# Modulation products half a tile behind their loads, the loads tied to the unit of weights at hand, and the gates' second bank from the common group

## The chip, the cores and the metric

The kernel runs on one core of one Trainium2 chip. The metric is device time in microseconds (us). Time before: 2287.91 us, the median of three runs (2285.56 to 2290.13). Engines are called as the profile calls them: PE (matrix products), PEld (its weight loads), DVE (elementwise), ACT (activations and casts), POOL (here small copies and the issue of some transfers) and SP (the issue of most transfers).

## The reference, cut to what matters

One layer works on 512 latent tokens x and 256 context tokens ctx, both of width 2048. A modulation vector is made from c by a matrix product with a large weight, `w_mod` (2048 x 12288). The normalised, modulated input goes through one combined projection `w_in`. Group A of its columns feeds a gated linear attention over chunks, forward and backward, whose start states come from the context; group B feeds a short convolution. Both are joined and go through an output projection, and a feed-forward block follows.

```python
m = silu(c) @ w_mod + b_mod          # six vectors of 2048: shift, scale, gate, twice
h = modulate(rmsnorm(x, norm1_g), shift1, scale1)
q, k, v, g, lf, lb, cb, cc, cx = split_proj(h @ w_in)
la_f = log_sigmoid(lf @ w_gate_f + b_gate_f) / 16     # la_b alike
o, _, _ = gla_bidir(q, k, v, la_f, la_b, s0_f, s0_b)  # s0 from the context tokens
x = x + gate1 * (concat(norm(o) * silu(g), cb * conv(cc * cx)) @ w_out)
x = x + gate2 * swiglu(modulate(rmsnorm(x, norm2_g), shift2, scale2))
```

Only the first two of the six vectors (4096 columns) are needed before the projection. The other 8192 columns of `w_mod`, 64 tiles of 128 rows by 2048, are worked off beside the projection and the attention, and are needed only after it.

## The kernel before, in words

**A unit of weights.** Weights of 32-bit floats are used as a high and a low part. A unit is 128 x 1024 numbers, 512 KB. `load_w` (from L125) loads it into a buffer of the group `raw` (L119 to L123, four buffers, issued by SP), ACT casts it to `whi` (L106), DVE subtracts to get `wlo` (L107); `whi` and `wlo` have three buffers each. `mm3` (L96) makes each product of three matmuls, so a unit is 24 matmuls of 128 x 512 in `proj_units` (from L499), which also remembers the present unit's `whi` in `unit`. Two units fill one accumulator.

**The modulation products.** `mod_some` (L380 to L409) works on the 128 half tiles, of 128 x 1024 and 512 KB each, of the rest of `w_mod`. For each, one transfer and one product with the broadcast silu(c) on DVE (L405), whose sum over the row is accumulated into a column of `modacc`, are written down. `behind` says how many half tiles the products stand behind their loads. At 0 the load takes a `raw` buffer on SP's queue, and the product is written right behind it. Above 0 the load is issued by POOL (L393, or L397), and ahead of it stands a copy of one column from the present unit's `whi` into the buffer (L392, or L396); the transfer overwrites it. The copy thus makes the transfer wait until that unit has been cast. Two thirds of these half tiles take one of two `wm` buffers, the others a `raw` buffer.

**The order of the work.** Code order sets each engine's queue, and a framework puts in the waits; each engine works its queue in order. `weave` (L564 to L570) takes stages in turn: one step of the stages, one unit of weights, then `mod_some` for 1.84 half tiles on the average.

- The context's states: `do_ctx` (from L518, six stages) with the four units of `do_q(0)` and `do_q(1)` (weights `wq`). Its last stages copy the start states (L551), on ACT or DVE as the framework chooses. Eleven half tiles, m0 to m10, are written here.
- The gates: `do_gates` (from L582), four stages tt0 to tt3. Each makes two gate tiles on PE in two banks `pzs` (forward, backward); `log_gates` (L489) then has ACT work through L493, L494 and L495, and DVE make the log gates (L497), which frees the banks. Beside them run the units of `do_g(0)` (four units of `wg`, G1 to G4) and `do_conv(0)` (from L681, six units of `wc`, C1 to C6). Eighteen half tiles, m11 to m28.
- The attention, head by head (`do_gla`, from L590), with the other units. Ahead of it stands `behind[0] = 2` (L705), so here POOL issues the transfers of half tiles.

The product of half tile mN is called pN below. The banks of 128 x 512 come from two groups: `bank` has five and `abank` three. The accumulators of the units are from `abank`, and so is the second `pzs` of a gate stage (L584).

Of the kernel before, what the change touches and what calls it, by code (L numbers as in the profile page):

```python
# [53 lines left out]
def tile_hybrid_block(  # L54
# [23 lines left out]
    def big(dtype=F32):  # L78
        return xpool.tile([P, SEQ], dtype, tag="t", name="big")
# [4 lines left out]
    def bank(name="bank"):  # L84
        return pspool.tile([P, 512], F32, tag="g", name=name, bufs=5)

    def abank(name="abank"):
        return pspool.tile([P, 512], F32, tag="a", name=name, bufs=3)
# [4 lines left out]
    def mm(o, l, r, start, stop):  # L93
        nc.tensor.matmul(o, l, r, start=start, stop=stop, skip_group_check=True)  # L94
# [24 lines left out]
    def load_raw(src):  # L119
        n = src.shape[-1]  # L120
        r = wpool.tile([P, 1024], F32, tag="raw", name="raw", bufs=4)
        nc.sync.dma_start(r[:, :n], src)
        return r[:, :n]  # L123
# [11 lines left out]
    def tok(t, tt):  # L135
        return t[:, tt * P : tt * P + P]
# [200 lines left out]
    def gate_rows(pz, half, d, a):  # L337

        q = slice(64 * half, 64 * half + 33)
        mm(pz, lfT[q, a : a + P], gatet[q, d, :], True, True)  # L340
# [35 lines left out]
    nmod, owed = [0], [0.0]  # L376

    pend, behind, unit = [], [0], []

    def mod_some(n, last):  # L380


        owed[0] += 2 * n
        while owed[0] >= 1 and (pend or nmod[0] < 2 * last):
            owed[0] -= 1
            if nmod[0] < 2 * last:
                j, hf = divmod(nmod[0], 2)
                src = wm2[j][:, hf * 1024 : hf * 1024 + 1024]
                if behind[0] and nmod[0] % 3:
                    w = gp.tile([P, 1024], F32, tag="wm", name="wm", bufs=2)  # L390

                    nc.gpsimd.tensor_copy(w[:, 0:1], unit[0])  # L392
                    nc.gpsimd.dma_start(w, src)  # L393
                elif behind[0]:
                    w = wpool.tile([P, 1024], F32, tag="raw", name="raw", bufs=4)
                    nc.gpsimd.tensor_copy(w[:, 0:1], unit[0])  # L396
                    nc.gpsimd.dma_start(w, src)  # L397
                else:
                    w = load_raw(src)
                pend.append((j, hf, w))  # L400
                nmod[0] += 1
                if len(pend) <= behind[0]:
                    continue
            j, hf, w = pend.pop(0)
            nc.vector.tensor_tensor_reduce(  # L405
                out=w, in0=w, in1=cbc[:, hf * 1024 : hf * 1024 + 1024], scale=1.0, scalar=0.0,
                op0=ALU.mult, op1=ALU.add, accum_out=modacc[:, j, hf : hf + 1])
# [81 lines left out]
    def log_gates(pool, tag, pzs, las):  # L489

        t = pool.tile([P, 2, 512], F32, tag=tag, name="lg")
        for i in range(2):
            nc.scalar.activation(t[:, i, :], pzs[i], AF.Abs)  # L493
        nc.scalar.activation(t, t, AF.Exp, scale=-1.0)  # L494
        nc.scalar.activation(t, t, AF.Ln, bias=onecol)  # L495
        for i in range(2):
            nc.vector.scalar_tensor_tensor(las[i], pzs[i], 0.0, t[:, i, :], op0=ALU.min, op1=ALU.subtract)  # L497

    def proj_units(acc, wsrc, x, units=(0, 1), part=ALL):  # L499

        for n, u in enumerate(units):
            w = load_w(wsrc[u], 8)
            unit[:] = [w[0][:, 0, 0:1].bitcast(F32)]
            for k in range(8):
                mm3(acc[:, part], sl(w, ALL, k), sl(x[8 * u + k], ALL, part), n == 0 and k == 0, n == 1 and k == 7)
            yield
# [5 lines left out]
    def do_q(h):  # L512
        acc = abank("acc")
        yield from proj_units(acc, wq[h], hx)
        q_t[h] = big()
        nc.scalar.activation(q_t[h], acc, AF.Copy, scale=QSCALE)

    def do_ctx():  # L518
        kds = [[], []]
        las = []  # L520
        for d in range(2):
            pzs = [bank("pzs") for _ in range(NCT)]
            for tt in range(NCT):
                gate_rows(pzs[tt], tt, d, SEQ + tt * P)
            las.append([big() for _ in range(NCT)])
            log_gates(hcpool, "lg", pzs, las[d])
            yield
        for d in range(2):
            for tt in range(NCT):
                pz = bank("pz")  # L530
                whole = tt == d
                mm(pz, cstt[:, B_SUFF + d, :], las[d][tt], True, not whole)
                if whole:
                    mm(pz, one16, las[d][1 - tt], False, True)
                tag, bufs = (("sq0", 2), (("lfs", "tm")[tt], 1))[d]
                e = hcpool.tile([P, 512], F32, tag=tag, name="kdc", bufs=bufs)
                nc.scalar.activation(e, pz, AF.Exp)
                nc.vector.tensor_tensor(e, e, kc[tt], op=ALU.mult)
                kds[d].append(e)
            yield  # L540
        S0[:] = [xpool.tile([P, 2, DV], F32, tag="t", name="s0") for h in range(HEADS)]
        for d in range(2):
            for hp in range(2):
                pz = bank("pz")
                for hh in range(2):
                    h = 2 * hp + hh
                    for tt in range(NCT):
                        mm(pz[:, hh * DV : hh * DV + DV], tok(kds[d][tt], h), vc[tt][hp][:, hh * DV : hh * DV + DV],
                           hh == 0 and tt == 0, tt == 1)
                for hh in range(2):  # L550
                    nc.any.tensor_copy(S0[2 * hp + hh][:, d, :], pz[:, hh * DV : hh * DV + DV])  # L551
            yield
# [11 lines left out]
    def weave(stages, fill):  # L564

        for _ in stages:
            next(fill, None)
            mod_some(MOD_STEP, 64)
        for _ in fill:
            mod_some(MOD_STEP, 64)  # L570

    weave(do_ctx(), (None for g in (do_q(0), do_q(1)) for _ in g))


# [6 lines left out]

    def do_gates():  # L582
        for tt in range(NX):
            pzs = [bank("pzs"), abank("pzs")]  # L584
            for d in range(2):
                gate_rows(pzs[d], d, d, tt * P)
            log_gates(hcpool, "lg", pzs, [las[0][tt], las[1][tt]])
            yield
# [92 lines left out]
    def do_conv(c):  # L681
# [17 lines left out]
        mix[8 + c] = y  # L699

    weave(do_gates(), (None for g in (do_g(0), do_conv(0)) for _ in g))
    es_hc.close()
    es_g = ExitStack()
    gp = es_g.enter_context(tc.tile_pool(name="gp", bufs=1, side="right"))
    behind[0] = 2  # L705
    for h in range(HEADS):
# [3 lines left out]
        if h + 2 < HEADS:  # L710
            fill.insert(0, do_q(h + 2))
        weave(do_gla(h), (None for g in fill for _ in g))
    mod_some(128, 64)
    mod_finish(0, 64)
    nc.vector.tensor_scalar(gsc2, modv[:, 32:48], 1.0, None, op0=ALU.add)
# [634 lines left out]
```

## Time and profile before

| what | us |
|---|---|
| median of three runs | 2287.91 (2285.56 to 2290.13) |
| the profiled execution, own time | 2285.08 |
| its span (first to last instruction) | 2283.3 |
| mean granted clock of PE | 0.996 |
| PE busy | 2233.8 (98%) |
| DVE busy | 1657.4 (73%) |
| ACT busy | 1003.3 (44%) |
| POOL busy | 248.4 (11%) |

The span is 1.8 us shorter than the execution's own time; the execution is 2.8 us under the median. In a row of the timeline stand the start in us from the span's start, the duration in us, engine, line, operation, what is written and read, sizes and a count; in square brackets the idle time of the engine just before it, and what ended it. In a row of the waits stand the engine, the tile and line that waited, who was waited for, the time in all, how often, and the longest. Matmuls overlap: their rows begin 0.23 us apart and are 0.39 us long.

### The profile page before, as it was taken

How to read it: one execution, taken by the hardware profiler on the slowest of the kernel's cores; microseconds unless marked ns; L12 is line 12 of the kernel's file. 1: busy time of each engine (PE TensorE's matmuls, PEld its weight loads, DVE VectorE, ACT ScalarE, POOL GpSimd, SP SyncE). 2: the span in 40 equal slices, each digit the busy share in tenths (PEclk: the TensorE clock that was granted, in tenths of full speed). 3: DMA queues.
4: the chain of work that ended last, by engine and by line, in shares of the span. 5: the costliest groups of instructions: out<-in, count | busy, mean ns of one | idle time of the engine just before them, and what ended most of it. 6: DMA issues, size and time to landing. Idle time of an engine off the chain costs nothing.

```text
span 2283.3 us, 28033 instructions
## 1 busy us (share of the span) xinstructions
PE 2233.8 (98%) x10276; PEld 1785.8 (78%) x10276; DVE 1657.4 (73%) x2069; ACT 1003.3 (44%) x1354; POOL 248.4 (11%) x396
## 2 busy tenths in 40 slices
PE   8999998999999999999999999999999999999997
PEld 4765666887788887777888888888888888888886
DVE  3566165565768646899788779878887887787885
ACT  3423155333233434665554455444545544433343
POOL 2433100222323000100000000000000000000000
PEclk9999999999999999999999999999999999999999
DMA  9683466565677354523643454354335596756752
GB/s 328 218 278 132 148 220 199 197 223 203 239 238 254 117 191 168 204 74 122 210 148 117 160 179 157 130 171 165 136 139 205 203 338 208 242 198 203 258 168 100
DMA packets 163410, 433.16 MB, mean 190 GB/s; under 512 B 18022, under 2 KB 38790, under 8 KB 163144
## 3 DMA queue, kind: packets, MB, share of 16 engines
q1 hardware_dynamic: 128984, 331.20, 43.4%
q0 software_dynamic: 22416, 78.66, 9.8%
q10 hardware_dynamic: 11872, 21.52, 2.5%
q8 instruction: 81, 1.33, 0.2%
q14 instruction: 57, 0.47, 0.1%
HBM read 380.95 MB, written 50.35 MB: 189 GB/s over the span
## 4 chain that ended last, share of the span: by engine, by line
issue 56%; POOL 2%; PE 1%; DVE 1%; ACT 0%; DMA 0%; POOLq 0%; DVEq 0%; ACTq 0%
POOL opd L1070 2%; PE acc L94 1%; DVE wlo L107 0%; DVE ch L849 0%; ACT y L1217 0%; DMA out<-g 0%; DVE u L1023 0%; POOL xnd L1026 0%; ACT whi L106 0%; POOL hbig L962 0%; DVE hbig L1024 0%; DVE u L869 0%; POOLq L1070 0%; ACT acc L1208 0%; DVE g L1205 0%
## 5 line engine op out<-in xcount | busy, mean ns | idle before, releaser
L106 ACT CAST whi<-ch 128x1024 fp32r<-128x1024 f32 x335 | 353.1, 1055 | 407.5 <-PE acc L94 343.3
L107 DVE TENSOR_TENSOR wlo<-ch,whi 128x1024 fp32r<-128x1024 f32 x335 | 407.6, 1221 | 122.7 <-ACT whi L106 121.9
L106 ACT CAST whi<-raw 128x1024 fp32r<-128x1024 f32 x258 | 271.0, 1052 | 455.9 <-PE acc L94 287.9
L107 DVE TENSOR_TENSOR wlo<-raw,whi 128x1024 fp32r<-128x1024 f32 x258 | 316.2, 1226 | 197.6 <-ACT whi L106 191.6
L94 PE MATMUL acc<-hhl,whi 128*128 128x512 f32 x640 | 199.1, 392 | 0.0
L94 PE MATMUL acc<-hhi,wlo 128*128 128x512 f32 x320 | 133.0, 417 | 11.8 <-DVE wlo L107 5.6
L94 PEld LDWEIGHTS acc<-hhl,whi 128*128 128x128 f32 x640 | 120.2, 188 | 27.3 <-issue 2.5
L1070 POOL DMA_DIRECT2D opd<-ol x80 | 43.3, 541 | 880.2 <-DVE ol L107 880.0
L405 DVE CUSTOM_DVE_ANT_0 wm<-wm,cbc 128x1024 f32<-128x1024 f32 x66 | 80.6, 1224 | 79.4 <-DMA wm<-wm 78.5
L94 PE MATMUL acc<-wlo,a6h 128*128 128x512 f32 (+1 forms) x330 | 127.4, 386 | 1.2 <-DVE wlo L107 1.2
L94 PE MATMUL acc<-wlo,a0h 128*128 128x512 f32 x324 | 127.5, 394 | 0.8 <-DVE wlo L107 0.8
L94 PE MATMUL acc<-whi,a6l 128*128 128x512 f32 (+1 forms) x330 | 127.1, 387 | 0.3 <-DVE v L869 0.3
L94 PE MATMUL acc<-whi,a6h 128*128 128x512 f32 (+1 forms) x330 | 127.2, 386 | 0.0
L94 PE MATMUL acc<-hhl,wlo 128*128 128x512 f32 x320 | 126.5, 395 | 0.0
L94 PE MATMUL acc<-whi,a5h 128*128 128x512 f32 x324 | 126.3, 390 | 0.0
L94 PE MATMUL acc<-hlo,whi 128*128 128x512 f32 x320 | 126.1, 394 | 0.2 <-DVE hlo L112 0.2
L94 PE MATMUL acc<-whi,a0h 128*128 128x512 f32 x324 | 126.2, 390 | 0.0
L94 PE MATMUL acc<-whi,a5l 128*128 128x512 f32 x324 | 126.2, 389 | 0.0
L94 PE MATMUL acc<-wlo,a5h 128*128 128x512 f32 x324 | 126.1, 389 | 0.0
L94 PE MATMUL acc<-whi,a0l 128*128 128x512 f32 x324 | 126.0, 390 | 0.0
L94 PE MATMUL acc<-hhi,whi 128*128 128x512 f32 x320 | 125.7, 393 | 0.0
L405 DVE CUSTOM_DVE_ANT_0 raw<-raw,cbc 128x1024 f32<-128x1024 f32 x62 | 75.4, 1222 | 49.0 <-DMA raw<-wm 48.8
(334 smaller groups left out, 4986.0 us busy)
## 6 DMA issues: line engine op xcount, KB each, us to landing
raw<-wu SPq DMA_DIRECT2D x92, 512.0 KB, 4.3
ch<-wu SPq DMA_DIRECT2D x88, 512.0 KB, 3.8
wm<-wm POOLq DMA_DIRECT2D x66, 512.0 KB, 5.4
raw<-wd SPq DMA_DIRECT2D x50, 512.0 KB, 5.8
raw<-wc SPq DMA_DIRECT2D x48, 512.0 KB, 4.9
opd<-oh ACTq DMA_DIRECT2D x80, 256.0 KB, 3.5
opd<-ol POOLq DMA_DIRECT2D x80, 256.0 KB, 3.9
ch<-wd SPq DMA_DIRECT2D x38, 512.0 KB, 4.3
```

What stands on the lines that cost most here:

```text
L94: nc.tensor.matmul(o, l, r, start=start, stop=stop, skip_group_check=True)
L106: nc.scalar.copy(hi, src)
L107: (eng or nc.vector).tensor_tensor(lo, src, hi, op=ALU.subtract)
L405: nc.vector.tensor_tensor_reduce(out=w, in0=w, in1=cbc[:, hf * 1024 : hf * 1024 + 1024], scale=1.0, scalar=0.0, op0=ALU.mult, op1=ALU.add, ...
L1070: nc.gpsimd.dma_start(opd[j][i, 1].rearrange("p k t -> p (k t)"), lo.bitcast(F32))
```

## The change

```diff
@@ mod_some @@
-                if behind[0] and nmod[0] % 3:
+                if behind[0] > 1 and nmod[0] % 3:
                     w = gp.tile([P, 1024], F32, tag="wm", name="wm", bufs=2)
...
                 elif behind[0]:
                     w = wpool.tile([P, 1024], F32, tag="raw", name="raw", bufs=4)
                     nc.gpsimd.tensor_copy(w[:, 0:1], unit[0])
                     nc.gpsimd.dma_start(w, src)
@@ ahead of the context's states @@
+    behind[0] = 1
     weave(do_ctx(), (None for g in (do_q(0), do_q(1)) for _ in g))
@@ do_gates @@
-            pzs = [bank("pzs"), abank("pzs")]
+            pzs = [bank("pzs") for _ in range(2)]
```

From the context's states to the attention `behind` is 1. The 29 loads m0 to m28 leave SP's queue for POOL's, each behind a copy from the present unit's `whi`; all still take `raw` buffers, of which there are four as before. Each product stands one half tile behind its load, p28 in the attention. The second bank of each gate stage comes from `bank`. Behind the new line all line numbers are one higher.

SP's queue in the gates' stages, of the kernel before: units (`wg`, `wc`) and half tiles (`wm2`).

```order
L122 DMA raw_2790<-wg 128x1024
L122 DMA raw_2820<-wm2 128x1024
L122 DMA raw_2823<-wm2 128x1024
L122 DMA raw_2837<-wg 128x1024
L122 DMA raw_2867<-wm2 128x1024
L122 DMA raw_2870<-wm2 128x1024
L122 DMA raw_2876<-wc 128x1024
```

The same place of the changed kernel, from G3 (`raw_2803`) on.

```order
L122 DMA raw_2803<-wg 128x1024
L122 DMA raw_2852<-wg 128x1024
L122 DMA raw_2893<-wc 128x1024
L122 DMA raw_2931<-wc 128x1024
L122 DMA raw_2972<-wc 128x1024
```

And POOL's queue there; in the kernel before POOL has nothing in this stretch. `whi_2805` is G3, `whi_2854` is G4, and `raw_2833` to `raw_2886` are m14 to m17.

```order
L396 COPY raw_2833<-whi_2805 128x1
L396 COPY raw_2837<-whi_2805 128x1
L397 DMA raw_2833<-wm2 128x1024
L397 DMA raw_2837<-wm2 128x1024
L396 COPY raw_2882<-whi_2854 128x1
L396 COPY raw_2886<-whi_2854 128x1
L397 DMA raw_2882<-wm2 128x1024
L397 DMA raw_2886<-wm2 128x1024
```

The half tiles moved from SP to POOL, mostly in pairs, each pair behind the cast of the unit then at hand; SP's queue holds units alone.

DVE's queue ahead of the log gates of tt0 (the two rows of L497), before: `raw_2820` to `raw_2909` are m14 to m19, `wlo_2793` is G3. The short instruction that reads the sum out behind each product is left out here and below.

```order
L405 ISA raw_2820,modacc_76<-raw_2820,cbc_79 128x1024
L107 TENSOR_TENSOR wlo_2793<-raw_2790,whi_2792 128x1024
L405 ISA raw_2823,modacc_76<-raw_2823,cbc_79 128x1024
L405 ISA raw_2867,modacc_76<-raw_2867,cbc_79 128x1024
L405 ISA raw_2870,modacc_76<-raw_2870,cbc_79 128x1024
L405 ISA raw_2906,modacc_76<-raw_2906,cbc_79 128x1024
L405 ISA raw_2909,modacc_76<-raw_2909,cbc_79 128x1024
L497 SCALAR_TENSOR_TENSOR hbig_2676<-pzs_2684,lg_2688 128x512
L497 SCALAR_TENSOR_TENSOR hbig_2680<-pzs_2685,lg_2688 128x512
```

And changed: `wlo_2806` is G3, `raw_2785`, `raw_2833` and `raw_2837` are m13, m14 and m15, `wlo_2855` is G4.

```order
L551 COPY s0_2634<-pz_2643 128x256
L107 TENSOR_TENSOR wlo_2806<-raw_2803,whi_2805 128x1024
L405 ISA raw_2785,modacc_76<-raw_2785,cbc_79 128x1024
L405 ISA raw_2833,modacc_76<-raw_2833,cbc_79 128x1024
L405 ISA raw_2837,modacc_76<-raw_2837,cbc_79 128x1024
L497 SCALAR_TENSOR_TENSOR hbig_2686<-pzs_2694,lg_2698 128x512
L497 SCALAR_TENSOR_TENSOR hbig_2690<-pzs_2695,lg_2698 128x512
L107 TENSOR_TENSOR wlo_2855<-raw_2852,whi_2854 128x1024
```

Four products, p16 to p19, moved from ahead of the log gates of tt0 to behind them; p15 is now the last one ahead. One copy of the start states moved from ACT to DVE.

DVE's queue over the last units of the convolution, before: `wlo_3029` is C5 and `wlo_3065` C6, `raw_3059` to `raw_3095` are m26 to m28.

```order
L405 ISA raw_3059,modacc_76<-raw_3059,cbc_79 128x1024
L405 ISA raw_3092,modacc_76<-raw_3092,cbc_79 128x1024
L107 TENSOR_TENSOR wlo_3029<-raw_3026,whi_3028 128x1024
L405 ISA raw_3095,modacc_76<-raw_3095,cbc_79 128x1024
L107 TENSOR_TENSOR wlo_3065<-raw_3062,whi_3064 128x1024
```

And changed: `wlo_3053` is C5 and `wlo_3091` C6; `raw_3036` and `raw_3040` are m23 and m24, `raw_3080` and `raw_3084` are m25 and m26, whose loads are tied to C5.

```order
L405 ISA raw_3036,modacc_76<-raw_3036,cbc_79 128x1024
L107 TENSOR_TENSOR wlo_3053<-raw_3050,whi_3052 128x1024
L405 ISA raw_3040,modacc_76<-raw_3040,cbc_79 128x1024
L405 ISA raw_3080,modacc_76<-raw_3080,cbc_79 128x1024
L405 ISA raw_3084,modacc_76<-raw_3084,cbc_79 128x1024
L107 TENSOR_TENSOR wlo_3091<-raw_3088,whi_3090 128x1024
```

Ahead of the subtraction of C6 now stand three products, two of them of half tiles whose loads wait for the cast of C5.

## The prediction

> **What bounds the kernel now.** I read the page first, then the busy time by stretches around the change, then the waits of that stretch, then the timelines of the engines that wait there. The page shows what the kernel is made of.
>
> ```profile
> span 2283.3 us, 28033 instructions
> PE 2233.8 (98%) x10276; PEld 1785.8 (78%) x10276; DVE 1657.4 (73%) x2069; ACT 1003.3 (44%) x1354; POOL 248.4 (11%) x396
> ```
>
> PE is busy for 98% of the span, so only its gaps and its clock can give anything back: 2283.3 - 2233.8 = 49.5 us in all. The change touches the stretch from the context's states (about 290 us) to the first attention head. The stretches of it that differ, with PE's busy time first and the granted clock behind the five engines:
>
> ```profile
> 350.00:360.00 10.00, 7.63 (x26) 4.26 (x24) 5.46 (x9) 1.67 (x3) 0.00 (x0) 0.92 0.66 208
> 360.00:370.00 10.00, 4.55 (x14) 3.52 (x14) 3.66 (x6) 9.90 (x11) 0.00 (x0) 0.56 0.47 160
> ```
>
> PE has one hole, at 355 to 370 us, and in it the clock falls to 0.56. The waits of 290 to 428 us name what it waits for, and what that waits for in turn.
>
> ```profile
> DVE raw L405 <- DMA raw<-wm: 24.7, 12, 4.2
> PE acc L94 <- DVE hbig L497: 5.5, 1, 5.5
> PE pzs L94 <- DVE hbig L497: 2.4, 1, 2.4
> ```
>
> PE waits for the log gates, and DVE for half tiles, 24.7 us in all. The timelines of PE, DVE and ACT show the chain.
>
> ```profile
> 354.76 1.12 PE L94 MATMUL pzs<-gatet,lfT 33*128 33x512 f32 x2
> 358.25 1.90 PE L94 MATMUL pzs<-gatet,lfT 33*128 33x512 f32 x2 [2.37 <-DVE hbig L497]
> 365.60 0.79 PE L94 MATMUL acc<-hhi,wlo 128*128 128x512 f32 x1 [5.45 <-DVE hbig L497]
> 373.77 0.50 PE L94 MATMUL acc<-hhi,wlo 128*128 128x512 f32 x1
> 384.80 0.39 PE L94 MATMUL acc<-hhi,wlo 128*128 128x512 f32 x1
> 390.24 0.39 PE L94 MATMUL acc<-hhi,wlo 128*128 128x512 f32 x1
> ```
>
> ```profile
> 353.17 1.23 DVE L405 CUSTOM_DVE_ANT_0 raw<-raw,cbc 128x1024 f32<-128x1024 f32 x1 [2.50 <-DMA raw<-wm]
> 355.76 1.22 DVE L405 CUSTOM_DVE_ANT_0 raw<-raw,cbc 128x1024 f32<-128x1024 f32 x1 [1.36 <-DMA raw<-wm]
> 356.91 1.28 DVE L497 SCALAR_TENSOR_TENSOR hbig<-pzs,lg 128x512 f32<-128x512 f32 x2
> ```
>
> ```profile
> 315.37 1.04 ACT L106 CAST whi<-raw 128x1024 fp32r<-128x1024 f32 x1
> 339.08 1.05 ACT L106 CAST whi<-raw 128x1024 fp32r<-128x1024 f32 x1 [3.27 <-DMA raw<-wg]
> 346.72 1.15 ACT L495 ACTIVATE lg<-lg,cidt 128x1024 f32<-128x1024 f32 x1
> 358.31 1.08 ACT L493 ACTIVATE lg<-pzs 128x512 f32<-128x512 f32 x2 [9.14 <-DVE hbig L497]
> 363.07 1.15 ACT L495 ACTIVATE lg<-lg,cidt 128x1024 f32<-128x1024 f32 x1
> ```
>
> The log gates of tt0 could start on DVE when ACT is done, at 346.72 + 1.15 = 347.87. They start at 356.91, since p16 to p19 stand ahead and wait for their transfers. PE's second gate bank of tt2 waits for them (2.37), ACT starts the next gates at 358.31 (9.14 idle), and the accumulator of G3, in the same group as the second banks, waits for those of tt1 (5.45).
>
> **What the removed hole is worth.** A unit takes 390.24 - 384.80 = 5.44 us. Without waits G4 would begin at 354.76, two gate tiles 1.06, a unit 5.44, the accumulator's change 0.09, two gate tiles 1.06 later, at 362.41. It begins at 373.77. The stretch loses 11.4 us, the half clock included. That is the most that the gates can give, 0.5%. Both edits reach for it: only p15 and older stand ahead of tt0's log gates, and the accumulator is out of the gates' group.
>
> **What the change adds.** SP loads only units now, and no half tile stands ahead of them in its queue. But the four buffers `raw` are still shared, so a unit's load waits for the product that frees its buffer (G1 for p7, G3 for p11, C4 for p20, C5 for p22), or for a `wlo`; the product waits for its transfer, and that for the cast of an earlier unit. A circle closes: cast, copy on POOL, transfer, product, load, cast. The attention of the kernel before shows its first links, on ACT, POOL and DVE:
>
> ```profile
> 447.63 1.03 ACT L106 CAST whi<-raw 128x1024 fp32r<-128x1024 f32 x1
> ```
>
> ```profile
> 411.03 1.05 POOL L393 DMA_DIRECT2D wm<-wm  x2
> 448.72 1.35 POOL L392 COPY wm<-whi 128x1 f32<-128x1 f32 x2 [12.30 <-ACT whi L106]
> 450.37 0.53 POOL L393 DMA_DIRECT2D wm<-wm  x1 [0.29 <-POOL wm L392]
> 451.28 0.53 POOL L393 DMA_DIRECT2D wm<-wm  x1 [0.38 <-issue]
> ```
>
> ```profile
> 417.01 1.23 DVE L405 CUSTOM_DVE_ANT_0 wm<-wm,cbc 128x1024 f32<-128x1024 f32 x1 [4.82 <-DMA wm<-wm]
> 419.46 1.23 DVE L405 CUSTOM_DVE_ANT_0 wm<-wm,cbc 128x1024 f32<-128x1024 f32 x1 [0.61 <-DMA wm<-wm]
> 454.57 1.23 DVE L405 CUSTOM_DVE_ANT_0 wm<-wm,cbc 128x1024 f32<-128x1024 f32 x1 [4.65 <-DMA wm<-wm]
> ```
>
> From the cast's end (447.63 + 1.03) to the first issue of a pair is 450.37 - 448.66 = 1.7 us; for a single half tile I take 1.0. From issue to landing is 454.57 - 450.37 = 4.2 or 417.01 - 411.03 = 6.0; I take 4.9, between them and nearer the smaller, whose copy waits for a cast as the new ones do. The second of a pair lands 451.28 - 450.37 = 0.9 to 419.46 - 417.01 = 2.4 later; I take 2.0, near the landing seen. Transfers by queue and kind at 280 to 430 us, the last column from issue to landing:
>
> ```profile
> raw<-wm SPq DMA_DIRECT2D x29, 512.0 KB, 4.8
> raw<-wc SPq DMA_DIRECT2D x6, 512.0 KB, 4.3
> raw<-wm POOLq DMA_DIRECT2D x2, 512.0 KB, 6.2
> ```
>
> A unit's load I take at 4.6, between 4.3 and 4.8. So the circle is 1.0 + 4.9 + 1.23 + 4.6 + 1.05 = 12.8 us with a single half tile, and 1.7 + 6.9 + 1.23 + 4.6 + 1.05 = 15.5 through the second of a pair. It feeds the unit two further on, and PE needs 2 x 5.44 = 10.88 for two. A circle longer than that starves PE wherever no `wlo` shortens it. [...]
>
> **The walk, on the clock of this profile.** The second `wq` unit's cast ends at 315.37 + 1.04 = 316.4, and m5 to m7 are tied to a unit cast about there: landings near 323, 325, 326. p7 stands behind log-gate and context products that wait for ACT, and ends by my estimate at 329.4. G1 loads until 334.0, its cast ends at 335.1; m11 lands 1.0 + 4.9 later at 341.0, p11 ends at 342.2, G3 loads until 346.8, and its cast ends at 347.9. Before it ended at 340.1. G3's cast stands on ACT ahead of the last start-state copies and the gates of tt0, so these run late: the copies to 349.7, the log gates' ACT part (4.7 to 5.9, the latter from 358.31 to 363.07 + 1.15) to about 355.0. Then m14 and m15, tied to G3: 347.9 + 1.7 + 4.9 = 354.5 and 356.5, p15 ends at 357.8, and tt0's first log gate is done at 358.5, though fewer products stand ahead of it.
>
> Stalls of PE that this adds, by the same walk from unit to unit:
>
> - tt1's second gate bank waits for the last start-state copy: 1.3.
> - tt2's second gate bank (ready at 354.76 + 1.3 + 0.5 = 356.6, waits for 358.5): 1.9, and with the clock 2.2.
> - tt3, behind tt1's log gates: 0.4.
> - C2 0.6 and C3 2.4: C3's load waits for `wlo` of C2, at 378.2; + 4.6 + 1.05 + 1.23 and a product ahead on DVE gives 386.0, where PE is free at 383.6.
> - C4 1.0 and C5 0.5: p22 is tied to C3's cast.
> - C6 4.0: m25 and m26 are tied to C5's cast, ending at 396.9. They land at 403.5 and 405.5, p26 ends at 406.7, and `wlo` of C6 behind it at 407.9, where PE is free at 403.9.
>
> Sum 12.4. In the kernel before, C6's subtraction ran 9 us ahead of its matmuls:
>
> ```profile
> 397.08 1.22 DVE L107 TENSOR_TENSOR wlo<-raw,whi 128x1024 fp32r<-128x1024 f32 x1
> 406.56 0.39 PE L94 MATMUL acc<-hhi,wlo 128*128 128x512 f32 x1
> ```
>
> The lead that fed the attention goes too. SP's timeline shows the next head's units issued from 394.92 us on, ahead of C6's matmuls:
>
> ```profile
> 394.92 2.61 SPq L122 DMA_DIRECT2D raw<-wq  x2
> 398.34 27.21 SPq L122 DMA_DIRECT2D raw<-wg  x4
> ```
>
> Now the first of them waits for p26 at 406.7 and is ready at 406.7 + 4.6 + 1.05 + 1.23 = 413.6, where C6 ends at 407.9 + 5.44 = 413.3; the later ones follow in turns of up to 15.5 against 10.88. I take 3.0, between 0.3 (the first alone) and 4.6 + 0.3 (one turn more).
>
> Nothing else costs time: POOL's 29 copies and issues run on an engine that is 11% busy, the start-state copy on DVE stands behind p11, beside transfers waited for anyway, and after the last product the totals of DVE's work are the same.
>
> Sum: -11.4 + 12.4 + 3.0 = +4.0 us. Against the profiled execution (2285.08, its span plus 1.8) that is 2289.1; on the median of three, 2287.91 + 4.0 = 2291.9. With the fast ends (4.2, 0.9, units 4.3) the stalls shrink to about 6.2, C6's to 1.9 and C3's to 0.6, and with the entry covered the sum is -5. With the slow ones (6.0, 2.4, units 4.8) each of the three larger stalls grows by some 1.7, and the sum is about +9. A measurement of this kernel can tell about 0.2%, 4.6 us, from no change.
>
> **The rivals.** A, faster: the landings are at their quick ends, and the gates' gain is kept. For it speaks that SP's half tiles no longer compete in one queue with the units, and the quick 4.2 above; against it, the POOL queue's 6.2. Time: 2287.9 - 5.2 = 2282.7. Chance 0.20.
>
> B, slower by more: each of the three gaps of about 2 us and more (tt2, C3, C6) also brings a stretch at half clock. A gap of 2.19 us elsewhere did:
>
> ```profile
> 1003.44 0.69 PE L94 MATMUL acc<-whi,a1l 128*128 128x512 f32 x1 [2.19 <-DVE a1l L107]
> 1003.93 0.63 PE L94 MATMUL acc<-wlo,a1h 128*128 128x512 f32 x1
> 1004.36 0.63 PE L94 MATMUL acc<-whi,a1h 128*128 128x512 f32 x1
> 1006.92 0.43 PE L94 MATMUL acc<-whi,a1h 128*128 128x512 f32 x1
> ```
>
> Matmuls began 0.43 us apart instead of 0.23 until 1006.9, 3.4 us at half speed, so 1.7 us lost each time. With three such windows, +4.0 + 5.1 = +9.1: 2297.0. It decides where the transfers are late enough for the gaps to stay over 2 us. Against it: the loss in a window is partly absorbed, since a slower PE lets the loads catch up. Chance 0.20. [...]
>
> C, the change doesn't do what it says: the log gates of tt0 start at 357 as before, only behind p14 and p15 tied to G3, the hole keeps its size, and the later stalls are swallowed by the same loss. Within 1 us of 2287.9. For it speaks that the walk has tt0's first log gate at 357.8 against 356.91. Chance 0.15.
>
> **How the numbers follow.** The forecast, +4.0, with its own range of 0 to +9 (2287.9 to 2297), has 0.45. Faster by over 0.2%: most of A (0.18) and a tail of the forecast (0.04): 0.22. Within: C (0.15) and the half of the forecast up to +4.6 (0.25): 0.40. Slower: the rest of the forecast and B: 0.38. The range reaches from A (2282.0) to just above B (2299.0).
>
> **What would show it.** Right: the hole at 355 to 370 us is gone or half as large, SP's unit loads wait for DVE's products, PE has new gaps ahead of C3 and C6 named after `wlo`, DVE ahead of those waits for `wm` transfers, and the first units of the attention arrive late. Wrong: C1 to C6 run without gaps and the stretch to 412 us ends 5 us or more earlier (A); or the clock row falls below 0.9 in the units of the convolution (B); or tt2 waits for L497 as long as before (C).

## The result and the profile after

The changed kernel takes 2301.05 us, the median of five runs (2297.12 to 2303.26), against 2287.91 for the kernel before: 13.1 us more. The ratio of the runs is 1.0062 with a 95% interval of 1.0049 to 1.0075 (the quotient of the two medians is 1.0057). The forecast was 2291.9 with a range from 2282.0 to 2299.0. The direction was right, the size was not: +13.1 where +4.0 was said, above rival B's +9.1 too.

The profiled execution, first the page's span and busy times:

```profile
span 2297.8 us, 28097 instructions
PE 2241.3 (98%) x10276; PEld 1789.5 (78%) x10276; DVE 1658.0 (72%) x2070; ACT 1003.1 (44%) x1353; POOL 292.0 (13%) x454
```

The span grew by 14.5 us and PE's busy time by 7.5, with as many matmuls: half of the loss is gaps, and half matmuls that took longer. The stretches that were shown of before, and three later ones that are full (10.00, clock 1.00) in the kernel before:

```profile
350.00:360.00 10.00, 8.07 (x30) 5.11 (x29) 4.09 (x8) 6.25 (x9) 4.05 (x7) 0.96 0.53 157
360.00:370.00 10.00, 9.81 (x28) 6.56 (x30) 5.07 (x8) 9.07 (x11) 0.55 (x2) 0.70 0.48 159
...
400.00:410.00 10.00, 5.91 (x25) 4.43 (x24) 4.41 (x8) 1.05 (x1) 4.35 (x7) 1.00 0.43 157
410.00:420.00 10.00, 9.15 (x45) 7.77 (x45) 6.24 (x10) 1.05 (x1) 2.06 (x6) 0.83 0.78 271
...
430.00:440.00 10.00, 6.15 (x23) 4.63 (x22) 7.33 (x14) 2.92 (x5) 1.62 (x2) 0.89 0.35 120
```

In the hole at 350 to 370 us PE now idles 2.1 us instead of 7.8, but the granted clock is still 0.70 in its second half; two new holes stand at 406 to 411 and at 433 to 437. PE's timeline at the marks that a comparison can use: first gate tile of tt0, second gate bank of tt2, gate tiles of tt3, the units C3 to C6, the first transpose of the attention (L595), its first `wg` unit, two waits behind it, and the first of the head's last products.

```profile
343.02 1.13 PE L94 MATMUL pzs<-gatet,lfT 33*128 33x512 f32 x4
360.19 2.07 PE L94 MATMUL pzs<-gatet,lfT 33*128 33x512 f32 x2 [2.12 <-DVE hbig L497]
369.64 1.13 PE L94 MATMUL pzs<-gatet,lfT 33*128 33x512 f32 x4
387.83 0.50 PE L94 MATMUL acc<-hhi,wlo 128*128 128x512 f32 x1 [0.50 <-DVE wlo L107]
394.36 0.50 PE L94 MATMUL acc<-hhi,wlo 128*128 128x512 f32 x1 [0.76 <-DVE wlo L107]
400.51 0.50 PE L94 MATMUL acc<-hhi,wlo 128*128 128x512 f32 x1 [0.38 <-DVE wlo L107]
410.85 0.80 PE L94 MATMUL acc<-hhi,wlo 128*128 128x512 f32 x1 [4.56 <-DVE wlo L107]
417.83 0.60 PE L595 MATMUL pk<-cidt,big 128*128 128x128 f32 x4
436.80 0.50 PE L94 MATMUL acc<-hhi,wlo 128*128 128x512 f32 x1 [3.85 <-DVE wlo L107]
...
454.76 1.13 PE L94 MATMUL pd<-vx,kk 128*128 128x256 f32 x4 [1.66 <-DVE hbig L633]
457.40 0.70 PE L94 MATMUL po<-sm,qe 128*128 128x256 f32 x2 [1.51 <-ACT sm L647]
...
478.21 1.89 PE L94 MATMUL po<-vx,big 128*128 128x256 f32 x8
```

And the same marks of the kernel before that were not shown yet:

```profile
341.24 1.13 PE L94 MATMUL pzs<-gatet,lfT 33*128 33x512 f32 x4
...
372.71 1.13 PE L94 MATMUL pzs<-gatet,lfT 33*128 33x512 f32 x4
...
412.00 0.60 PE L594 MATMUL pk<-cidt,big 128*128 128x128 f32 x4
...
463.28 1.89 PE L94 MATMUL po<-vx,big 128*128 128x256 f32 x8
```

These marks cut the loss into three. Gates, tt0 to tt3: 31.47 us before, 26.62 after, a gain of 4.85. Convolution, tt3 to the first transpose: 39.29 before, 48.19 after, a loss of 8.90. First head, up to its last products: 51.28 before, 60.38 after, a loss of 9.10. Together +13.15; the first 341 us differ by 1.8, the rest by -0.4. So the gain at the gates is there, the convolution gives back nearly twice as much, and the entry into the attention costs as much again.

DVE's timeline at these two places: the subtractions of C5, of C6 and of the attention's third unit, g1 (the first of `wg`; its second unit, Q2, is the second of `wq`), with the products of half tiles ahead of C6 and g1.

```profile
399.23 1.23 DVE L107 TENSOR_TENSOR wlo<-raw,whi 128x1024 fp32r<-128x1024 f32 x1 [2.86 <-ACT whi L106]
...
407.16 1.23 DVE L405 CUSTOM_DVE_ANT_0 raw<-raw,cbc 128x1024 f32<-128x1024 f32 x1 [5.56 <-DMA raw<-wm]
408.42 1.22 DVE L405 CUSTOM_DVE_ANT_0 raw<-raw,cbc 128x1024 f32<-128x1024 f32 x1
409.57 1.22 DVE L107 TENSOR_TENSOR wlo<-raw,whi 128x1024 fp32r<-128x1024 f32 x1
...
432.63 1.23 DVE L405 CUSTOM_DVE_ANT_0 wm<-wm,cbc 128x1024 f32<-128x1024 f32 x1 [7.25 <-DMA wm<-wm]
...
434.39 1.22 DVE L405 CUSTOM_DVE_ANT_0 wm<-wm,cbc 128x1024 f32<-128x1024 f32 x1
435.53 1.22 DVE L107 TENSOR_TENSOR wlo<-raw,whi 128x1024 fp32r<-128x1024 f32 x1
```

The casts of C5, C6, Q2 and g1 on ACT:

```profile
398.14 1.05 ACT L106 CAST whi<-raw 128x1024 fp32r<-128x1024 f32 x1 [7.70 <-DMA raw<-wc]
404.23 1.05 ACT L106 CAST whi<-raw 128x1024 fp32r<-128x1024 f32 x1 [5.03 <-DMA raw<-wc]
...
421.94 1.05 ACT L106 CAST whi<-raw 128x1024 fp32r<-128x1024 f32 x1 [7.72 <-DMA raw<-wq]
423.49 1.05 ACT L106 CAST whi<-raw 128x1024 fp32r<-128x1024 f32 x1 [0.50 <-DMA raw<-wg]
```

And POOL, tied to the casts of C5 and of Q2:

```profile
399.26 2.38 POOL L396 COPY raw<-whi 128x1 f32<-128x1 f32 x2 [7.36 <-ACT whi L106]
401.57 1.05 POOL L397 DMA_DIRECT2D raw<-wm  x2
...
423.05 2.38 POOL L392 COPY wm<-whi 128x1 f32<-128x1 f32 x2 [6.89 <-ACT whi L106]
425.37 1.05 POOL L393 DMA_DIRECT2D wm<-wm  x2
```

The circle can be read off. C5 is cast until 399.19; the pair tied to it is issued at 401.57 and its first half tile is there at 407.16; its two products stand ahead of C6's subtraction, so that ends at 410.8, though C6 was cast at 405.3. PE starts C6 at 410.85, 4.56 late. The same again one stage on: Q2 is cast until 423.0, the pair tied to it is issued at 425.37 and lands at 432.63, and g1's subtraction stands behind both products. g1 had been cast at 424.5; its subtraction runs at 435.53, 11 us later.

### The profile page after: what moved, and what is told of

It reads as the page before. It is cut to its first block, busy times and chain, and to the rows that moved or that the text cites. A ratio compares the mean times of both kernels' runs of the same rounds, so it can differ in the third digit from the quotient of the medians.

```text
span 2297.8 us, 28097 instructions
## 1 busy us (share of the span) xinstructions
PE 2241.3 (98%) x10276; PEld 1789.5 (78%) x10276; DVE 1658.0 (72%) x2070; ACT 1003.1 (44%) x1353; POOL 292.0 (13%) x454
## 4 chain that ended last, share of the span: by engine, by line
issue 55%; POOL 2%; PE 1%; DVE 1%; ACT 0%; DMA 0%; POOLq 0%; DVEq 0%; ACTq 0%
POOL opd L1071 2%; PE acc L94 1%; DVE wlo L107 0%; DVE ch L850 0%; ACT y L1218 0%; DMA out<-g 0%; DVE u L1024 0%; POOL xnd L1027 0%; ACT whi L106 0%; POOL hbig L963 0%; DVE hbig L1025 0%; DVE u L870 0%; POOLq L1071 0%; ACT acc L1209 0%; DVE g L1206 0%
## 5 line engine op out<-in xcount | busy, mean ns | idle before, releaser
L405 DVE CUSTOM_DVE_ANT_0 wm<-wm,cbc 128x1024 f32<-128x1024 f32 x66 | 80.6, 1223 | 79.0 <-DMA wm<-wm 78.2
```

The source lines that it names most:

```text
L405: nc.vector.tensor_tensor_reduce(out=w, in0=w, in1=cbc[:, hf * 1024 : hf * 1024 + 1024], scale=1.0, scalar=0.0, op0=ALU.mult, op1=ALU.add, ...
```

## The experiments

Theory 1: the tie closes a circle (cast, copy, transfer, product, unit's load, cast) that feeds units more slowly than PE uses them, so the units' lead is used up and PE waits. Theory 2: the products standing one half tile later hold the four buffers longer, or POOL's queue is slow; the tie itself is nothing. The last column is the ratio to the kernel before on the same chip, the others are us. The three stretches are those above.

| run | gates | convolution | first head | ratio, 95% interval |
|---|---|---|---|---|
| before | 31.47 | 39.29 | 51.28 | 1 |
| changed | 26.62 | 48.19 | 60.38 | 1.0062 (1.0049 to 1.0075) |
| e1 banks only | 25.91 | 39.49 | 54.58 | 0.9987 (0.9977 to 0.9996) |
| e2 on SP, not tied | 26.30 | 43.04 | 51.78 | 0.9989 (0.9980 to 0.9998) |
| e3 on POOL, not tied | 28.47 | 47.11 | 51.54 | 1.0015 (1.0003 to 1.0026) |
| e4 tied to m17 | 22.74 | 49.16 | 52.36 | 1.0003 (0.9993 to 1.0013) |
| e5 banks as before | 31.17 | 43.12 | 61.92 | 1.0067 (1.0050 to 1.0084) |
| e6 tied from m18 | 20.26 | 50.22 | 55.30 | 1.0006 (0.9993 to 1.0019) |
| e7 tied to m24 | 24.90 | 44.08 | 55.48 | 1.0021 (1.0011 to 1.0031) |
| e8 tied, no lag | 23.94 | 50.84 | 61.82 | 1.0056 (1.0039 to 1.0074) |
| e9 m31, m32 not tied | 26.04 | 48.34 | 51.91 | 1.0016 (1.0005 to 1.0028) |
| e10 none in gates | 20.27 | 43.17 | 50.07 | 1.0008 (0.9999 to 1.0018) |
| e11 none in gates, banks as before | 27.86 | 39.30 | 50.07 | 1.0049 (1.0037 to 1.0061) |
| e12 tied m18 to m21 | 20.26 | 44.29 | 57.95 | 0.9990 (0.9981 to 0.9999) |

The stretches come from one profiled execution each. Those of one kernel differ by a few us: e1 and e2 were built with nearly the same order on every engine, and their three stretches sum to 119.98 and 121.12, but split differently.

**e1, the banks alone.**

```diff
-    behind[0] = 1
+    behind[0] = 0
```

> Theory 1 (the tie closes a circle: cast, copy, transfer, product, unit's load, cast): the banks alone carry the gain at the gates, and nothing is lost later, since no half tile is tied. The wait of the accumulator of G3 for the log gates (5.45 us) and most of the half clock behind it go; the wait of 2.37 us stays, as p16 to p19 still stand ahead of the log gates of tt0. 4 to 9 us faster than before. Theory 2 (the loss comes from the products standing one half tile later, which holds the four buffers longer, or from POOL's queue): the same here, 4 to 9 us faster. A rival to both: the second gate bank in the group of five takes a bank that the gates of the stage before hold, and PE waits as long as before: within 2 us of before.

Measured 2283.01 against 2285.44, 2.4 us faster: the sign as expected by both theories, the size under it. The gates gain 5.6 us, and the wait of the accumulator is gone; the wait for the log gates of tt0 stays (1.34), and the gates take 25.91 us where e6, without a wait there, takes 20.26. So a gain of the changed kernel's size at the gates comes with the banks alone. The first head takes 3.3 us more, with waits of 0.80 and 1.51 us that neither theory has.

**e2, the loads on SP and not tied.**

```diff
-                elif behind[0]:
+                elif behind[0] > 1:
```

> Products one half tile behind, banks changed, but the 29 loads stay on SP's queue and are not tied to a unit. Theory 1: the conv units C2 to C6 and the entry into the attention run without waits of over 0.5 us, the gates keep their gain: 3 to 9 us faster than before. Theory 2, holding buffers longer: most of the loss stays, 8 to 13 us slower than before, with waits of PE for wlo ahead of C6 and in the first head.

2281.49 against 2285.44: 4.0 us faster by the medians, 2.5 by the ratio, at the lower edge of theory 1's 3 to 9, and with the loss gone altogether. One wait of 1.83 us stands in the convolution, where theory 1 had none over 0.5. Theory 2 in its form about the buffers falls.

**e3, the loads on POOL and not tied.**

```diff
-                    nc.gpsimd.tensor_copy(w[:, 0:1], unit[0])
+                    if behind[0] > 1:
+                        nc.gpsimd.tensor_copy(w[:, 0:1], unit[0])
                     nc.gpsimd.dma_start(w, src)
```

> As the changed kernel, loads on POOL's queue, but without the copy from the present unit: a load waits for its buffer alone. Theory 1: faster than before by 0 to 8 us, no wait of over 1 us ahead of C6. Theory 2 in the form that POOL's queue is slow (issue and landing of half tiles): 6 to 13 us slower than before, with landings of over 5 us and the wait ahead of C6 still there.

2288.73 against 2285.44, 3.3 us slower: between the theories. The first head is as in the kernel before (51.54), so the 9 us of the entry belong to the tie. The convolution loses 7.8, with waits of 2.46 and 2.66 us for `wlo`, and the log gates of tt0 come later (3.92). The framework built another order on DVE here, with five products ahead of them. Landings on POOL's queue were not slower here: the half tiles that are loaded into `raw` at 280 to 430 us take 5.1 us from issue to landing in the median, as in e2 on SP's queue. What then costs these 3.3 us, queue or order, wasn't told apart. Up to the first transpose this run is as late as the changed kernel: gates and convolution take 75.58 us together, 74.81 there and 70.76 before. So what these runs show of the tie alone is the entry; its part in the convolution is read off the trace.

**e4, tied up to m17 alone.**

```diff
-                elif behind[0]:
+                elif behind[0] > 1 or behind[0] and nmod[0] < 18:
```

> As the changed kernel up to m17 (context's states and gates), then m18 to m28 on SP's queue, not tied, still one behind. Theory 1: the stretch to tt3 as in the changed kernel, 3 us ahead of before there, C4 to C6 and the entry into the attention without waits: 0 to 5 us faster than before. Theory 2: the lag goes on, so the entry still loses: 6 to 13 us slower.

2286.44 against 2285.44: no difference. The gates gain 8.7, the entry is as before, both as theory 1 has it; but the convolution loses 9.9 in spite of untied loads, with waits of 1.67 and 4.11 us. The longer one is ahead of C3, whose cast starts on ACT at 384.30, behind the log gates of tt3: lateness made in the gates' stages is paid in the convolution.

**e5, the changed kernel with the gates' banks as before.**

```diff
-            pzs = [bank("pzs") for _ in range(2)]
+            pzs = [bank("pzs"), abank("pzs")]
```

> The changed kernel with the gates' second bank from abank again, as before. Theory 1 (the supply of units through the tied half tiles sets when the convolution ends, not PE): the accumulator of G3 waits for the log gates of tt1 again, 5 to 7 us, but the units are late anyway, so the stalls ahead of C2 to C6 shrink by as much, and the time is within 4 us of the changed kernel, 10 to 17 us slower than before. Rival (PE sets the end, the losses add): 18 to 22 us slower than before.

1.0067 against 1.0062 for the changed kernel: theory 1. The accumulator of G3 waits 5.28 us again, the gates lose their gain (31.17), and the convolution takes 43.12 in place of 48.19, since fewer of its waits are left. The subtraction of g1 ends 93.4 us after the first gate tile, in the changed kernel 93.7, without lag (e8) 93.9, in the kernel before 80.6. With the loads tied, the supply of units sets the time, not PE, and what PE gains at the gates it waits for later.

**e6, tied from m18 on.**

```diff
-                elif behind[0]:
+                elif behind[0] > 1 or behind[0] and nmod[0] >= 18:
```

> m0 to m17 on SP's queue and not tied, m18 to m28 tied on POOL's queue, as changed. Theory 1: the loss belongs to the convolution's half tiles and the entry behind them: the gates as in the untied run (26 us from the first gate to the last), the stalls ahead of C3 to C6 and the late units in the first head as changed; 7 to 14 us slower than before. Rival (the lateness is inherited from the context's states, where the first ties stand): within 4 us of before.

2286.76 against 2286.05: the rival's figure, and theory 1's was wrong. The convolution loses as much as in the changed kernel (50.22, 4.67 us ahead of C6), but the gates' hole is gone altogether:

```profile
355.67 1.13 PE L94 MATMUL pzs<-gatet,lfT 33*128 33x512 f32 x4
362.41 1.13 PE L94 MATMUL pzs<-gatet,lfT 33*128 33x512 f32 x4
```

tt2 and tt3 each run their two pairs of gate tiles without a wait, 20.26 us from tt0 to tt3. This is the whole 11.2 us of the hole, and the first head loses 4.0, not 9.1. That e4 and e6 cost nothing is a net result: they gain 8.7 and 11.2 us at the gates and lose 11.0 and 15.0 behind them. My reading is that the lead of the units is a store: the ties up to m17 use up one part of it, those from m18 another, and only both together empty it before the attention. The runs fit this, but none measures the lead itself.

**e7, tied up to m24.**

```diff
-                elif behind[0]:
+                elif behind[0] > 1 or behind[0] and nmod[0] < 25:
```

> As changed up to m24, then m25 to m28 on SP's queue, not tied: those that stand between C5, C6 and the first units of the attention. Theory 1, with the entry made by the last ties alone: the 4.6 us wait ahead of C6 and the 3.9 us wait in the first head go, the first head takes 51 to 54 us from its first transpose to its last products (60.4 as changed), and the kernel is 0 to 6 us slower than before. Rival (the whole chain is late, and the last four half tiles add nothing): 9 to 14 us slower, with the late wlo in the first head still there.

2290.29 against 2286.05, 4.2 us slower: theory 1. The wait ahead of C6 shrinks from 4.56 to 0.42, that for g1 from 3.85 to 0.81; the first head takes 55.48 us, a little over the 51 to 54 that were expected. Four ties less are worth some 9 us.

**e8, tied, the products right behind their loads.**

```diff
-                if len(pend) <= behind[0]:
+                if len(pend) <= (behind[0] if behind[0] > 1 else 0):
```

> Loads tied and on POOL's queue as changed, but each product written right behind its load instead of one half tile later. Theory 1 (the tie and the queue cost, the lag is nothing, since the framework places the products by its own estimate): within 4 us of the changed kernel, 9 to 16 us slower than before. Theory 2 (products one half tile later hold the buffers): within 4 us of before.

2298.14 against 2286.05, 1.0056: within a few us of the changed kernel. The lag, the first words of the change, costs and brings nothing here. The code does not set DVE's queue alone, as the description of the kernel before has it: the framework chooses where the products stand (that it goes by an estimate of when their data come was the author's supposition, and no run shows it). Without lag p15 still stands last ahead of the log gates of tt0; on SP with lag (e2) p16 to p19 stand ahead of them as before, and on POOL without the tie (e3) there are five products too. It was the tie that moved them.

**e9, the two half tiles ahead of g1 not tied.**

```diff
-                    nc.gpsimd.tensor_copy(w[:, 0:1], unit[0])
+                    if nmod[0] not in (31, 32):
+                        nc.gpsimd.tensor_copy(w[:, 0:1], unit[0])
                     nc.gpsimd.dma_start(w, src)
```

> The changed kernel, with the copies from the present unit left out for m31 and m32 alone, the two half tiles whose products stand on DVE right ahead of the subtraction of the attention's third unit (the first of wg). Theory 1 in its new form (the entry costs 9 us because these two products wait for transfers tied to the late cast of the second wq unit, and hold the subtraction): the 3.9 us wait of PE in the first head and the half clock behind it go, the first head takes 52 to 56 us from its first transpose to its last products (60.4 as changed), and the kernel is 5 to 9 us slower than before. Rival (the units themselves come late through the four buffers, whatever stands ahead on DVE): 11 to 14 us slower, the wait as long.

2289.28 against 2285.7, 3.6 us slower instead of 13.1, less than the 5 to 9 that were expected. The convolution is as in the changed kernel; PE has no wait for g1, and the first head takes 51.91 us. DVE ahead of g1's subtraction (L406 is the product):

```profile
421.41 1.23 DVE L107 TENSOR_TENSOR wlo<-raw,whi 128x1024 fp32r<-128x1024 f32 x1 [1.76 <-ACT whi L106]
...
423.99 1.23 DVE L406 CUSTOM_DVE_ANT_0 raw<-raw,cbc 128x1024 f32<-128x1024 f32 x1 [0.21 <-DMA raw<-wm]
425.24 1.23 DVE L406 CUSTOM_DVE_ANT_0 wm<-wm,cbc 128x1024 f32<-128x1024 f32 x1
...
426.99 1.22 DVE L107 TENSOR_TENSOR wlo<-raw,whi 128x1024 fp32r<-128x1024 f32 x1
```

Three products stand there again, but none waits for long: the wait of 7.25 us is gone, and g1's subtraction starts at 426.99 in place of 435.53. These two ties stand in the kernel before too, where they cost nothing; behind late units they make up most of the loss.

**e10 and e11, no half tiles beside the gate stages**, with the banks as changed and as before. In both the four stages write none, and seven move to later places.

```diff
-    def weave(stages, fill):
+    def weave(stages, fill, step=MOD_STEP):
 
         for _ in stages:
             next(fill, None)
-            mod_some(MOD_STEP, 64)
+            mod_some(step, 64)
...
-    weave(do_gates(), (None for g in (do_g(0), do_conv(0)) for _ in g))
+    weave(do_gates(), (None for g in (do_g(0), do_conv(0)) for _ in g), 0)
```

> No tie and no lag; banks as changed; no half tiles are written beside the four gate stages, so that seven of them move to later places. Theory: the log gates of tt0 no longer stand behind products that wait for transfers; the gates take 20 to 22 us from first to last gate (31.5 before), nothing is lost later, and the kernel is 7 to 12 us faster than before. Rival (the seven half tiles cost as much where they go, at the end of the attention): within 4 us of before.

> As the run without half tiles in the gates, with the second gate bank from the accumulators' group as before. Theory: with the log gates in time no accumulator waits for them, so the banks don't matter: within 3 us of that run. Rival (the group of three is too small whenever an accumulator and three gate banks meet): 4 to 7 us slower than that run.

e10: 2287.82 against 2285.7, the rival's case. Up to the last products of the first head it is 8.5 us ahead (113.51 against 122.04), with the hole gone (20.27). Then it gives that back. The products in `wm` buffers at 700 to 1000 us, of the kernel before:

```profile
L405 DVE CUSTOM_DVE_ANT_0 wm<-wm,cbc 128x1024 f32<-128x1024 f32 x13 | 15.9, 1222 | 6.4 <-DMA wm<-wm 5.7 <-POOL raw L396 0.4
```

And of e10:

```profile
L405 DVE CUSTOM_DVE_ANT_0 wm<-wm,cbc 128x1024 f32<-128x1024 f32 x16 | 19.6, 1223 | 20.4 <-DMA wm<-wm 20.1 <-POOL wm L392 0.3
```

The last one starts at 792.3 us in place of 760.3, and DVE waits 20.1 us for these transfers in place of 5.7. These rows are DVE's; PE's own waits at 480 to 1010 us grow by only some 4 us, so how the rest of the gain is lost stays open. e11: 2295.84, 8.0 us above e10, against the theory and above the rival's 4 to 7 too. The banks do matter where nothing is tied: the accumulator of G3 still waits 5.07 us for the log gates, though no gate bank waits for them any more. The other part is the end of the half tiles, where PE waits for the totals:

```profile
364.57 0.79 PE L94 MATMUL acc<-hhi,wlo 128*128 128x512 f32 x1 [5.07 <-DVE hbig L497]
...
807.37 0.59 PE L920 MATMUL ptr<-cidt,modv 128*16 128x128 f32 x2 [8.11 <-DVE big L698]
```

**e12, m18 to m21 tied alone.**

```diff
-                elif behind[0]:
+                elif behind[0] > 1 or behind[0] and 18 <= nmod[0] < 22:
```

> Only m18 to m21 tied and on POOL's queue, all others up to m28 on SP's queue. Theory (what helps at the gates is that the tie makes the framework place p18 and later behind the log gates; what costs is the number of ties in a row, which use up the units' lead): gates in 20 to 23 us as in the run tied from m18, convolution in 40 to 45 us, 3 to 9 us faster than before. Rival (each tie costs its full circle): 0 to 6 us slower than before.

2283.09 against 2285.7, 2.6 us faster, just short of the expected 3. The gates lose their hole as in e6; the convolution loses 5.0 and the first head 6.7, the latter with waits in its scan (2.94 and 1.51). e1, e2 and e12 all beat both kernels, by about 0.1%: less than the 0.2% that was called the measure of a difference, though their intervals end below 1.

## Why the prediction was wrong

**Right, by the changed profile and the experiments:** what the gates' hole is made of and worth (e6 and e10 take away 11.2 us of it where 11.4 was said); the circle and about its length (from C4's subtraction to C6's 16.5 us, C3's to C5's 12.7, where 12.8 to 15.5 was said); the walk up to the log gates of tt0 (said 357.8, measured 359.44, or 357.7 without the 1.8 us that the first 341 us are later); the wait ahead of C6 (4.0 said, 4.56 measured), with its place and cause. The added time of the convolution, 8.5 by the sum (0.6, 2.4, 1.0, 0.5, 4.0), was 8.9, but that it fits is in part luck: C2 and C3 together lost 0.7 us where 3.0 was said, and 1.5 us of half clock behind the wait for C6, which the sum doesn't have, made up for most of it. That the tie alone makes this loss isn't shown either, since e3 lost 7.8 us there without it.

**Wrong: the entry into the attention**, the term of 3.0 us "between 0.3 and 4.6 + 0.3". It measured 9.1, outside its own bounds, and e9 shows why: without two ties it is 0.6. The step counted when the units could be loaded and cast, and took the late ones to follow "in turns of up to 15.5". It did not follow DVE's queue into the attention, where two products of half tiles tied to Q2's cast stand ahead of the subtraction of g1. That order stood in the kernel before too, and cost nothing, since Q2 was cast until 407.81, 19.2 us before PE began g1 (426.96); both products were done and g1 subtracted at 421.83, 5.1 us ahead of PE. With the lead used up, the wait of 7.25 us on DVE reached PE: 3.85 us of the 9.1 are its wait for g1, 1.7 the half clock behind that, and two waits further on, of 1.66 and 1.51 us, which the kernel before doesn't have, are most of the rest. In e9 PE waits at none of these places for more than 0.4 us. The prediction had the time from cast to landing (1.7 + 4.9 us; here 432.63 - 423.0 = 9.6) and applied it to the products ahead of C6, but not to the next such pair.

**Under-counted: half clock**, which stood among the rivals; the sum had 0.3 us of it. Rival B had the mechanism and came near the price: three slow stretches, at tt2, C6 and g1 where tt2, C3 and C6 were said. The end of the one behind tt2, and the two behind the waits for C6 and g1:

```profile
366.13 0.40 PE L94 MATMUL acc<-hhl,wlo 128*128 128x512 f32 x1
...
411.44 0.63 PE L94 MATMUL acc<-hlo,whi 128*128 128x512 f32 x1
411.87 0.63 PE L94 MATMUL acc<-hhi,whi 128*128 128x512 f32 x1
...
413.93 0.40 PE L94 MATMUL acc<-hlo,whi 128*128 128x512 f32 x1
...
437.14 0.40 PE L94 MATMUL acc<-hlo,whi 128*128 128x512 f32 x1
...
441.25 0.39 PE L94 MATMUL acc<-hhi,wlo 128*128 128x512 f32 x1
```

Matmuls begin 0.43 us apart instead of 0.23, until 366.13, 413.93 and 441.25. The one at C6 costs 1.5 us (6.98 us from C6's start to the first transpose, 5.44 before), the one at g1 about 1.7 by the same measure as in the prediction (half of the some 3.4 us from 437.8 to 441.25). The one behind tt2 is dearer: from the second gate bank of tt2 to tt3 9.45 us pass (360.19 to 369.64), where e6 has 6.2 (6.74 from tt2 to tt3, less 0.53 between the two banks), so some 3.2 us are lost, at a granted clock of 0.70. That is 6.4 us in all, where B had 5.1. The argument against B, that a slower PE lets the loads catch up, did not hold at C6: the attention began later by its 1.5 us.

**The sum again with measured terms:** gates -4.85 where -11.4 + 3.9 = -7.5 was said (the half clock behind tt2, 0.3 in the sum, was some 3.2; smaller waits at tt1 and tt3 took part of that back), convolution +8.9 for +8.5, entry +9.1 for +3.0: +13.15 where +4.0 was said. Of the miss of 9.1 us the entry is 6.1. The prediction's chances hold a slip too: the rest of the forecast and B add up to 0.36, not 0.38.

**The rivals.** A is refuted: the pair tied to C5 landed 5.6 us after its issue, that tied to Q2 7.3, and DVE's waits on the way to C6 and g1 are those of slow landings. C is refuted too: the log gates start no earlier, but the accumulator no longer waits, and the gates are 4.85 us shorter.

## What to carry to other kernels

A load that is tied to the use of another load makes a circle; add its links up from the trace and compare the sum with what the fast engine uses in that time. As long as a lead was left a slower circle cost nothing (the ties of m31 and m32 in the kernel before, where g1 was ready 5.1 us ahead of PE), and parts of it measured one at a time can look harmless (e4 and e6: no difference each, as they gained at the gates what they lost later; together 13 us); so follow the lead, unit by unit, until the walk is past the last place that can empty it, through every queue that holds a waiting instruction ahead of the one that is wanted. PE, freed earlier at the gates (26.62 us in place of e5's 31.17), gained nothing by it where the supply of units set the end (1.0062 against 1.0067).

## What the runs showed of the hardware

Whether a gap of PE brought half clock was not set by its length alone. A gap of 2.40 us in e12 did not (granted clock 1.00 from 390 to 400 us):

```profile
392.99 0.50 PE L94 MATMUL acc<-hhi,wlo 128*128 128x512 f32 x1 [2.40 <-DVE wlo L107]
393.33 0.39 PE L94 MATMUL acc<-hlo,whi 128*128 128x512 f32 x1
```

One of 1.99 us in e10 did at once:

```profile
391.93 0.80 PE L94 MATMUL acc<-hhi,wlo 128*128 128x512 f32 x1 [1.99 <-DVE wlo L107]
392.53 0.63 PE L94 MATMUL acc<-hlo,whi 128*128 128x512 f32 x1
392.95 0.63 PE L94 MATMUL acc<-hhi,whi 128*128 128x512 f32 x1
```

Behind the gap of 3.85 us above PE began at full speed and slowed about 1 us later: the matmul at 437.14 is still 0.40 us long, those from 438.78 on are 0.63. The slow stretches of the changed kernel end at 366.1, 413.9 and 441.25 us. The one behind tt2 had lasted 5.9 us by then, counted from the second gate bank (360.19), the one at C6 3.1 us, counted from C6's start (410.85), and the one at g1 some 3.4 us, from 437.8. What sets where such a stretch begins and ends is not shown by these runs.
